# A hybrid attention and convolution layer: adaLN's first shift and scale by full precision products, later bias tables and convolution blocks, bias tiles read straight from the tables

## The chip, the cores and the metric

One core of a Trainium2 chip runs the kernel. The metric is the device time of one execution in microseconds; the kernel before took 2568.53 us, the median of three runs (2560.25 to 2570.44). All traces are of single executions on that core.

## What is computed

One layer of a diffusion backbone, in float32, for 2048 latent tokens of width 1024 and 256 context tokens. What matters here:

```python
mod_x = silu(c) @ w_ada + b_ada               # six rows of 1024: sh1, sc1, g1, sh2, sc2, g2
mod_c = silu(c_ctx) @ w_ada + b_ada
hx = rms_norm(x, norm1_g) * (1 + sc1) + sh1   # hc likewise from ctx, with mod_c
q, k, v, u = split(hx @ w_in)
attn = neighbourhood_attention(rope(q), q, rope(k), v, kc, vc, rpb)   # window + context keys, bias rpb
a, b = split(u); h = depthwise_conv31(a * sigmoid(b)) + dw_bias
conv = silu(layer_norm(h))
x = x + g1 * (concat(attn, conv) @ w_out)
x = x + g2 * (relu(modulate(rms_norm(x)) @ w1) ** 2 @ w2)
return rms_norm(x, final_g)
```

## The kernel before, in words

Every large product is made of three products of one pass (`mm3`, L89): each operand is split into a rounded part, made on ACT, and the rest, made by a subtraction on DVE or GpSimd (POOL in the profile); high times high, high times low and low times high are added in PSUM. PSUM is four tiles of 128 x 1024 (`psA`, L54), handed out in turn; a tile that is held longer is taken out of the turn.

**The head (L136 to L277).** The first two chunks of `w_ada`, shift and scale, come in four tiles of 2 MB each, in two loads each (`load_wada`); one row of `b_ada` each goes into `brow`. `silu(c)` and `silu(c_ctx)` are spread over 64 columns each, so one product with a 128 x 128 stationary matrix gives both rows on 64 partitions. First each bias row is multiplied with a row of ones at full precision (L193), then `ada_step` (L196) runs 8 times for the scale (`hf` 1) and 8 times for the shift: ACT casts 128 x 1024 of `w_ada`, DVE or POOL subtracts, and PE does six products of 512 columns. Between the shift's steps DVE builds `Ar` from the scale's PSUM and scales the first x tiles (L244, L251). After the last product the shift is copied out and added to the x tiles (L664 to L673), and PE transposes these (`trans`, L224, L227) for the projection.

**The projection (L559 to L881).** Two blocks of 1024 tokens; in each 10 groups of columns of `w_in` (4 `u`, 2 `q`, 2 `k`, 2 `v`), each in two halves of 512 tokens. So there are 40 steps: for the first block u is steps 0 to 7, q 8 to 11, k 12 to 15, v 16 to 19, for the second u 20 to 27, q 28 to 31, k 32 to 35, v 36 to 39. A step's products are 10.9 to 11.5 us of PE at the full clock. `half` (L710) emits a step: products, then what they need after: for u a sigmoid gate stored to `h_d`, for q and k the rotary work (`rope_store`: DVE, ACT, POOL, an `m1` buffer of two, stores), for v the split and stores (`v_tiles`). Beside this, the same function issues at fixed steps:

- the convolution by blocks of 98 tokens (`Conv`, L418), through a transform of length 128: `load` of 128 rows of `h_d` (`cw`), `split` (ACT, DVE), `fwd` (three products; `y` = PSUM times a table on DVE, into SBUF; `cyh` on ACT, `cyl` on DVE), one step later `inv` (six products, bias, statistics), two steps later `turn` (four transposes, activation, store). One PSUM tile is held for this. Block 0 enters at step 7 and one block at each further step to 16; blocks 10 to 20 enter at steps 27 to 37.
- the relative bias tables: `bias_start` and `bias_end` at step 6, one head in each of steps 8 to 15 (`bias_head`: two loads, a POOL add, four stores into `tf_d` and `ti_d`), and at steps 18, 20, 21 and 24 `bias_rows` (L302), which copies shifted pieces of both into `bias_d` in DRAM, 12 copies in all.
- the second x half of each block: loads, squares on ACT, scaling on DVE, shift on POOL (`norm_half`, L545), transposes (`trans_half`). For the second half of the second block the norm stands at step 20 and the transposes at step 22.
- three gate chunks of `w_ada` (`ada_chunk`, L484): 16 loads of 256 KB and 16 accumulations on DVE each, taken from a queue at a budget of 5.2 a step (0.6 each) in u steps, and `finish`, two steps after the last, which sums over partitions on PE, loads the bias row and adds it.

A planner orders the instructions of each engine by program order and a timeline of its own; where `in_order` is called, DVE, ACT and POOL keep the order written. All DMAs of these parts are issued on SP's queue.

**Attention (L898 to L1235).** 64 steps of 128 queries and two heads (4 pairs of heads, 8 groups of 4 rows, 2 halves of the columns). At each step `loads` issues k, q and v three or two steps ahead, and `load_b` (L998) one bias tile of 128 rows per head whenever the kind of group changes, 48 in all; eight of these at the start.

The output projection and the MLP follow; they are not touched.

## Time and profile before

| | us |
|---|---|
| median of three runs | 2568.53 |
| the profiled execution, its own time | 2570.69 |
| its span, first to last instruction | 2568.9 |
| PE busy in the span | 2430.5 |
| DVE, ACT, POOL busy | 1790.2, 1248.7, 1467.8 |

The span is divided as follows: head to about 52 us, projection to about 665, attention to about 940, then output projection and MLP. The profile gives busy times by engine; the granted clock of TensorE is 1.00 at 2.4 GHz and 0.50 at 1.2 GHz, and a stretch between these has had both. In the timeline a row in square brackets tells the idle time ahead and what ended it.

### The profile page before, as it was taken

To read this page: it belongs to the slowest core of one execution; us is meant where nothing else is said; L and a number is where in the kernel's file an instruction comes from. 1 tells how busy PE (TensorE), PEld (TensorE's weight loads), DVE (VectorE), ACT (ScalarE), POOL (GpSimd) and SP (SyncE) were. 2 spreads that over 40 slices of the span, in tenths; PEclk is the share of its full clock that TensorE was granted. 3 is DMA by queue.
4 is the path that set the end of the run, shared out by engine and by line. 5 is a ranking of instruction groups with operands and counts; after the bars stand their busy time and mean duration, and the time that the engine had idled before them with its cause. 6 is when DMAs were issued, how large, how long until landed. Compare 5 with 4: busy or idle time off the path is not lost.

```text
span 2568.9 us, 42313 instructions
## 1 busy us (share of the span) xinstructions
PE 2430.5 (95%) x15903; PEld 2216.9 (86%) x15903; DVE 1790.2 (70%) x2465; ACT 1248.7 (49%) x2162; POOL 1467.8 (57%) x1055
## 2 busy tenths in 40 slices
PE   7997989899889999988999999999999999999997
PEld 5985889689889999987998889999889998799996
DVE  6646743666689976468666697666786676876676
ACT  4334531443689963134444554444554445454442
POOL 3537422442578856457555676555675556755564
PEclk9998999999999999999999999999999999999999
DMA  8555764653899865665333443333343334433321
GB/s 299 158 168 163 223 216 130 196 154 110 227 253 262 241 182 174 195 231 165 99 99 107 129 139 111 101 105 99 121 148 101 99 99 126 137 107 100 105 92 57
DMA packets 293882, 387.26 MB, mean 151 GB/s; under 512 B 38021, under 2 KB 231228, under 8 KB 293644
## 3 DMA queue, kind: packets, MB, share of 16 engines
q1 hardware_dynamic: 293660, 384.54, 49.7%
q8 instruction: 125, 2.05, 0.3%
q14 instruction: 81, 0.66, 0.1%
q10 hardware_dynamic: 16, 0.00, 0.0%
HBM read 308.03 MB, written 86.76 MB: 154 GB/s over the span
## 4 chain that ended last, share of the span: by engine, by line
PE 62%; DVE 10%; DMA 9%; POOL 5%; issue 4%; SPq 2%; ACT 1%; DVEq 0%; POOLq 0%; ACTq 0%
PE pall L90 18%; PE pall L91 18%; PE pall L92 18%; PE pall L1105 2%; PE pall L1069 1%; PE pall L1030 1%; DVE s L1398 1%; DMA ar<-at_d 1%; DVE ac L1501 1%; DVE ac L1497 1%; PE pall L1107 1%; DVE w L1423 1%; PE pall L1032 1%; DMA cw<-h_d 1%; DMA xn_d<-xo 1%
## 5 line engine op out<-in xcount | busy, mean ns | idle before, releaser
L90 PE MATMUL pall<-w,hh 128*128 128x512 f32 x1024 | 406.0, 397 | 11.0 <-DVE ac L1497 7.2
L91 PE MATMUL pall<-w,hh 128*128 128x512 f32 x1024 | 403.0, 394 | 0.0
L92 PE MATMUL pall<-w,hl 128*128 128x512 f32 x1024 | 397.2, 392 | 0.6 <-DVE hl L1454 0.6
L1497 DVE TENSOR_TENSOR ac<-pall,ac 128x1024 f32<-128x1024 f32 x239 | 286.8, 1214 | 73.9 <-PE pall L92 73.2
L90 PEld LDWEIGHTS pall<-w,hh 128*128 128x128 f32 x1024 | 195.1, 190 | 51.6 <-issue 4.4
L92 PEld LDWEIGHTS pall<-w,hl 128*128 128x128 f32 x1024 | 193.3, 189 | 41.9 <-DVE hl L1454 2.2
L91 PEld LDWEIGHTS pall<-w,hh 128*128 128x128 f32 x1024 | 194.8, 190 | 36.4 <-issue 0.2
L1451 ACT ACTIVATE c<-c 128x512 f32<-128x512 f32 x128 | 80.9, 632 | 157.2 <-DVE c L1471 129.2
L86 POOL TENSOR_TENSOR w_0l<-w_0r,w_0h 128x1024 fp32r<-128x1024 f32 x20 | 50.7, 2537 | 172.7 <-ACT w_0h L85 152.5
L90 PE MATMUL pall<-xah,w 128*128 128x256 f32 x512 | 144.8, 284 | 4.7 <-ACT w L1392 4.7
L92 PE MATMUL pall<-xah,w 128*128 128x256 f32 x512 | 145.2, 284 | 0.0
L91 PE MATMUL pall<-xal,w 128*128 128x256 f32 x512 | 145.0, 283 | 0.0
L1454 DVE TENSOR_TENSOR hl<-c,hh 128x512 fp32r<-128x512 f32 x128 | 123.7, 967 | 15.3 <-ACT hh L1453 15.2
L1062 POOL TENSOR_SCALAR sb<-sb,ri 128x696 f32<-128x696 f32 (+1 forms) x128 | 105.6, 826 | 49.7 <-DVE ri L1057 40.7
L1044 DVE CUSTOM_DVE_ANT_0 sb<-pall,bias 128x696 f32<-128x696 f32 (+1 forms) x128 | 108.0, 845 | 6.5 <-PE pall L1032 5.9
L1052 ACT ACTIVATE sb<-sb,mn 128x696 f32<-128x696 f32 (+1 forms) x128 | 109.6, 857 | 0.6 <-DVE mn L1044 0.6
L90 PEld LDWEIGHTS pall<-xah,w 128*128 128x128 f32 x512 | 98.1, 192 | 7.5 <-ACT w L1392 4.9
L91 PEld LDWEIGHTS pall<-xal,w 128*128 128x128 f32 x512 | 98.6, 192 | 2.8
L92 PEld LDWEIGHTS pall<-xah,w 128*128 128x128 f32 x512 | 98.6, 192 | 2.1
L90 PE MATMUL pall<-xth,w 128*128 128x256 f32 x256 | 75.2, 294 | 19.1 <-DVE pu L1459 19.1
L1105 PE MATMUL pall<-pw,v 120*128 120x256 f32 (+1 forms) x480 | 90.8, 309 | 0.8 <-ACT ob L1112 0.8
L1081 DVE TENSOR_TENSOR pw<-pall,pw 120x512 fp32r<-120x512 f32 (+1 forms) x128 | 83.5, 653 | 5.1 <-ACT pw L1076 4.7
(853 smaller groups left out, 8797.0 us busy)
## 6 DMA issues: line engine op xcount, KB each, us to landing
v<-v_d SPq DMA_DIRECT2D x144, 120.0 KB
q<-q_d SPq DMA_DIRECT2D x64, 256.0 KB
wr<-in_w_ada SPq DMA_DIRECT2D x48, 256.0 KB
v_d<-vt SPq DMA_DIRECT2D x64, 160.0 KB
wa<-in_w_ada SPq DMA_DIRECT2D x8, 1024.0 KB
x<-in_x SPq DMA_DIRECT2D x16, 512.0 KB
kr<-k_d SPq DMA_DIRECT2D x32, 256.0 KB
at_d<-ao SPq DMA_DIRECT2D x32, 256.0 KB
```

Source lines behind the costliest of these rows:

```text
L86: (eng or GE).tensor_tensor(l, r, f(h), ALU.subtract)
L90: TE.matmul(outp, lh, rh, start=start, stop=False)
L91: TE.matmul(outp, lh, rl, start=False, stop=False)
L92: TE.matmul(outp, ll, rh, start=False, stop=stop)
L1044: VE.tensor_tensor_reduce(sb[:, c0:SE_], d["s"][:, 512 - SC0 + c0:768], bt[:, c0:SE_], -1.0, 3e38, ALU.add, ALU.min, mn)
L1052: SE.activation(pb[:, c0:SE_], pb[:, c0:SE_], AF.Exp, bias=d["mn"], scale=-1.0, accum_out=d["sm"])
L1062: GE.tensor_scalar(pb[:, c0:SE_], pb[:, c0:SE_], d["ri"], 1.0, ALU.mult, ALU.mult)
L1081: VE.tensor_tensor(pw[0:120, 0:nch, 1, :], d["tv"], f(pw)[0:120, 0:nch, 0, :], ALU.subtract)
L1105: TE.matmul(o, VT[(pr, *key)][0:n, hd, :], pw[0:n, ch, :, :], start=(ch == 0), stop=False)
L1451: SE.activation(c, c, AF.Relu)
L1454: VE.tensor_tensor(dl, cv, f(dh), ALU.subtract)
L1497: VE.tensor_tensor(ac, po_, ac, ALU.add)
```

## The change

It does six things. (1) The head's products take `silu(c)` and `w_ada` as they are, in float32 at full precision, two instructions for each of the 16 steps, with no casts and subtractions of `w_ada`; the bias rows are split instead, and added by products of one pass (`ada_bias`). (2) The convolution's blocks enter by a table of steps (`ENTER`): 0 to 7 at steps 12 to 19, 8 at 22, 9 at 24, 10 to 20 at 27 to 37 as before; u steps can run `inv` and `turn` too. (3) `y` lies in a PSUM tile of the common turn. (4) The bias tables start at step 17 (`G0 - 2` is group 8) and are made in steps 20 to 27; `bias_d` and its 12 copies are gone, and `load_b` reads a bias tile by four loads of 32 rows out of `tf_d` or `ti_d`. (5) A gate chunk's bias row is loaded with the last accumulation. (6) The last half's odd x tiles are shifted on DVE.

```diff
-    silh = pa.tile([P, KD, P], F32R, tag="cos", name="silh")
-    sill = pa.tile([P, KD, P], F32R, tag="sin", name="sill")
...
-    VE.tensor_copy(sv_[0], silb)
-    VE.tensor_tensor(sv_[1], silb, f(sv_[0]), ALU.subtract)
+    silr = pa.tile([P, KD, P], F32, tag="cos", name="silr")
+    VE.tensor_copy(silr.rearrange("p k (j n) -> p k j n", j=2), silb)
+    brh, brl = ([wtile(f"br{z}{hf}")[0:1] for hf in range(2)] for z in "hl")
+    onesr = wtile("onesr")[0:1, 0:P]
+    VE.tensor_copy(onesr, ones[0:1, :])
     for hf in (1, 0):
+        SE.copy(brh[hf], brow[hf])
+        VE.tensor_tensor(brl[hf], brow[hf], f(brh[hf]), ALU.subtract)
+
+    def ada_bias(hf):
         for n in range(2):
-            TE.matmul(pm[hf][:, n * 512:(n + 1) * 512], ones[0:1, :], brow[hf][:, n * 512:(n + 1) * 512],
-                      start=True, stop=False)
+            sl = slice(n * 512, (n + 1) * 512)
+            TE.matmul(pm[hf][:, sl], onesr, brh[hf][:, sl], start=True, stop=False)
+            TE.matmul(pm[hf][:, sl], onesr, brl[hf][:, sl], start=False, stop=False)
 
     def ada_step(hf, k):
         src = wts[hf, k // 4][:, k % 4, :]
-        wh, wl = wtile(f"wah{k}{hf}"), wtile(f"wal{k}{hf}")
-        SE.copy(wh, src)
-        (GE if k % 3 == 1 else VE).tensor_tensor(wl, src, f(wh), ALU.subtract)
         for n in range(2):
             sl = slice(n * 512, (n + 1) * 512)
-            o = pm[hf][:, sl]
-            TE.matmul(o, silh[:, k, :], wh[:, sl], start=False, stop=False)
-            TE.matmul(o, sill[:, k, :], wh[:, sl], start=False, stop=False)
-            TE.matmul(o, silh[:, k, :], wl[:, sl], start=False, stop=(k == KD - 1))
+            TE.matmul(pm[hf][:, sl], silr[:, k, :], src[:, sl], start=False, stop=(k == KD - 1))
...
-    def bias_rows(i):
-        for ty, t, o, n in ((0, tf_d, 7 - i, 320), (1, ti_d, 3 - i, 440), (2, tf_d, 3 - i, 320)):
-            SY.dma_start(bias_d[ty][:, i], t.rearrange("h f c n -> (h f) c n")[:, :, o * 40:o * 40 + n])
...
-            y = pa.tile([P, 2, 512], F32, tag="acc", bufs=2, name=f"cy{i}")
+            y = psA(f"cy{i}").rearrange("p (z n) -> p z n", z=2)
...
+    def conv_at(d):
+        i = ENTER.get(now[0] - d)
+        if i is not None:
             (Conv.inv, Conv.turn)[d - 1](cvs[i])
...
             if i == 2 * KD:
+                box["b"] = pa.tile([1, D], F32, tag="m1", bufs=2, name=f"br{ch}")
+                SY.dma_start(box["b"], a["b_ada"][:, ch * D:(ch + 1) * D])
                 pe_todo.append(finish)
...
-            shift(i)
+            shift(i, VE if b and hf and i % 2 else GE)
...
+    ENTER = {n: i for i, n in enumerate([*range(12, 20), 22, 24, *range(27, 38)])}
...
             for t in range(4):
+                if t % 2 == 0:
+                    conv_at(2 - t // 2)
...
-        if gi == 3 and hf == 0:
+        if gi == G0 - 2 and hf == 1:
             bias_start()
             bias_end()
-        if 4 <= gi < 8:
-            bias_head((gi - 4) * 2 + hf)
+        if G0 <= gi < G0 + 4:
+            bias_head((gi - G0) * 2 + hf)
...
-        SY.dma_start(bt[:, SC0 - nw:SC0], bias_d[ty][h * 2 + hf].rearrange("i c n -> (i c) n"))
+
+        t, o = ((tf_d, 7), (ti_d, 3), (tf_d, 3))[ty]
+        for i in range(4):
+            SY.dma_start(bt[i * 32:i * 32 + 32, SC0 - nw:SC0], t[h, hf][:, (o - i) * 40:(o - i) * 40 + nw])
```

## Rows read from the trace of the kernel before

**Rows 1.** The page, busy time of each engine: us, share of the span, instructions.

```profile
PE 2430.5 (95%) x15903; PEld 2216.9 (86%) x15903; DVE 1790.2 (70%) x2465; ACT 1248.7 (49%) x2162; POOL 1467.8 (57%) x1055
```

**Rows 2.** Stretches of 20 us: engine busy times, granted clock, DMA share, GB/s.

```profile
0.00:20.00 20.00, 14.07 (x24) 7.35 (x25) 6.99 (x8) 7.70 (x9) 5.51 (x8) 1.00 0.90 344
...
200.00:220.00 20.00, 15.96 (x64) 12.61 (x65) 13.31 (x19) 13.30 (x27) 14.15 (x12) 0.91 0.68 187
220.00:240.00 20.00, 15.16 (x68) 11.88 (x66) 11.33 (x15) 8.04 (x17) 13.83 (x5) 0.93 0.39 99
240.00:260.00 20.00, 10.94 (x30) 8.00 (x31) 15.21 (x9) 7.72 (x13) 18.39 (x12) 0.56 0.57 169
260.00:280.00 20.00, 20.00 (x92) 16.33 (x91) 18.82 (x20) 9.15 (x14) 10.41 (x6) 1.00 0.70 185
...
300.00:320.00 20.00, 18.18 (x145) 17.50 (x144) 8.61 (x17) 11.34 (x20) 2.04 (x1) 1.00 0.96 319
...
360.00:380.00 20.00, 15.02 (x116) 14.20 (x115) 10.83 (x8) 9.34 (x14) 8.60 (x3) 0.93 0.37 106
380.00:400.00 20.00, 18.68 (x136) 18.66 (x135) 5.18 (x5) 5.63 (x6) 6.43 (x4) 0.82 0.05 14
...
420.00:440.00 20.00, 20.00 (x169) 20.00 (x168) 10.54 (x11) 3.19 (x4) 5.22 (x2) 1.00 0.48 133
...
480.00:500.00 20.00, 11.83 (x47) 7.24 (x46) 15.74 (x24) 10.92 (x22) 17.71 (x10) 0.92 0.64 193
```

**Rows 3.** Timeline of PE in the head: start, duration, operation, count, idle time ahead.

```profile
6.18 3.75 PE L193 MATMUL pall<-brow,ones 1*128 1x512 f32 x4 [3.42 <-DMA brow<-in_b_ada]
...
42.55 1.17 PE L206 MATMUL pall<-wal,silh 128*128 128x512 f32 x2 [2.69 <-DVE wal L200]
...
46.50 0.39 PE L204 MATMUL pall<-wah,silh 128*128 128x512 f32 x1
...
47.66 0.39 PE L206 MATMUL pall<-wal,silh 128*128 128x512 f32 x1
51.83 0.66 PE L227 MATMUL pall<-ident,x 128*128 128x128 f32 x4 [3.78 <-DVE x L666]
```

**Rows 4.** The tile `wa`, operations on it: ns least, median, most; first and last start.

```profile
L199 ACT CAST wah<-wa x16: 1032/1044/1055, 6.4 to 36.9; 128x1024 fp32r<-128x1024 f32 x16
L200 DVE TENSOR_TENSOR wal<-wa,wah x10: 1209/1612/3389, 7.5 to 43.8; 128x1024 fp32r<-128x1024 f32 x10
...
L200 POOL TENSOR_TENSOR wal<-wa,wah x6: 2358/2428/3403, 8.5 to 38.0; 128x1024 fp32r<-128x1024 f32 x6
```

**Rows 5.** Timeline of PE in the MLP: the gate's two products at full precision.

```profile
1401.23 1.88 PE L1370 MATMUL pall<-fg,ones 128*128 128x512 f32 x4
```

**Rows 6.** Timeline of DVE in the head: two scalings of x tiles.

```profile
46.12 4.21 DVE L251 SCALAR_TENSOR_TENSOR x<-x,ss,Ar 128x1024 f32<-128x1024 f32 x2
```

**Rows 7.** Timelines of PE, DVE and POOL about the longest wait in the q steps.

```profile
251.94 0.74 PE L91 MATMUL pall<-cyl,chl 128*98 128x512 f32 x1 [6.50 <-DVE cyl L439]
...
242.54 9.34 DVE L439 TENSOR_TENSOR cyl<-cy,cyh 128x1024 fp32r<-128x1024 f32 x1 [5.82 <-ACT cyh L438]
...
240.18 9.27 POOL L221 TENSOR_TENSOR x<-x,Br 128x1024 f32<-128x1024 f32 x4
```

**Rows 8.** Timelines of DVE and POOL: norm of the last x half.

```profile
370.04 9.04 DVE L218 SCALAR_TENSOR_TENSOR x<-x,n11ss,Ar 128x1024 f32<-128x1024 f32 x4
...
371.40 12.20 POOL L221 TENSOR_TENSOR x<-x,Br 128x1024 f32<-128x1024 f32 x4 [18.04 <-DVE x L218]
```

**Rows 9.** Stretches of 20 us, as rows 2, at attention's first change of heads.

```profile
720.00:740.00 20.00, 15.66 (x123) 15.18 (x122) 15.46 (x42) 14.54 (x33) 13.95 (x23) 0.97 1.04 247
```

**Rows 10.** Waits from 455 to 505 us: who for whom, us, times, longest.

```profile
PE pall L90 <- DVE br L518: 5.3, 1, 5.3
```

**Rows 11.** The tile `bias`: its loads in attention, ns least, median, most.

```profile
L1008 SPq DMA_DIRECT2D bias<-bias_d x48: 326/353/1444, 651.9 to 879.2; - x48
```

**Rows 12.** Waits from 640 to 690 us.

```profile
DVE kt L842 <- DMA kr<-k_d: 4.2, 1, 4.2
```

More of the change, by code (lines that the diff above doesn't have):

```diff
@@ L111, in hybrid_layer @@
     ti_d = dr.tile([8, 2, 32, 14 * 40], F32, name="ti_d")
-    bias_d = [dr.tile([16, 4, 32, n], F32, name=f"bias_d{i}") for i, n in enumerate((320, 440, 320))]
     ident = const.tile([P, P], F32, name="ident")
@@ L251, in scale0 @@
         VE.scalar_tensor_tensor(x0[i], x0[i], ss0[:, i:i + 1], Ar, ALU.mult, ALU.mult)
+    ada_bias(1)
     for k in range(KD):
         ada_step(1, k)
+    ada_bias(0)
     TE.transpose(pk[:, 144:152], vrow, ident[:8, :8])
@@ L464, in hybrid_layer, with conv_end @@
     cvs = [Conv(i) for i in range(NCB)]
-    cv_pos = [0]
-    def conv_at(d, last):
-        i = cv_pos[0] - d
-        if 0 <= i < last and not hasattr(cvs[i], f"did{d}"):
-            setattr(cvs[i], f"did{d}", True)
+    now = [0]
+    def conv_at(d):
+        i = ENTER.get(now[0] - d)
+        if i is not None:
             (Conv.inv, Conv.turn)[d - 1](cvs[i])
-    def conv_end(last):
-        i = cv_pos[0]
-        if i < last:
+    def conv_end():
+        i = ENTER.get(now[0])
+        if i is not None:
             cvs[i].split()
             cvs[i].fwd()
-            if i + 1 < last:
-                cvs[i + 1].load()
-        cv_pos[0] += 1
+        i = ENTER.get(now[0] + 1)
+        if i is not None:
+            cvs[i].load()
     def ada_chunk(ch):
@@ L515, in finish @@
                           start=True, stop=True)
-            br = pa.tile([1, D], F32, tag="m1", bufs=2, name=f"br{ch}")
-            SY.dma_start(br, a["b_ada"][:, ch * D:(ch + 1) * D])
+            br = box["b"]
             VE.tensor_tensor(br, pg[0:1, :], br, ALU.add)
@@ L679, in hybrid_layer @@
     NG = len(groups)
-    CB0 = (BLK - P + PAD) // CL + 1
-    CBS = (CB0, NCB)
-    BR0 = 9
+    G0 = NG // NB
+    ENTER = {n: i for i, n in enumerate([*range(12, 20), 22, 24, *range(27, 38)])}
+    assert len(ENTER) == NCB
     adas = {ch: ada_chunk(ch) for ch in (2, 3, 4)}
-    G0 = NG // NB
     ADA = {G0 - 1: 2, G0: 3, G0 + 2: 4}
@@ L727, in half @@
             SY.dma_start(h_d[t0:t0 + 512, ct * P:(ct + 1) * P].rearrange("(t p) c -> p t c", p=P), sg)
-            if ct == 3 and hf == 1:
-                cv_pos[0] = (0, CB0)[b]
-                cvs[cv_pos[0]].load()
-                conv_end(CBS[b])
+            conv_end()
         elif kind in "qk":
@@ L734, in half @@
             for j in range(2):
-                conv_at(2 - j, CBS[b])
+                conv_at(2 - j)
                 for k in range(KD):
@@ L739, in half @@
             rope_store(b, kind, idx, hf, pt)
-            conv_end(CBS[b])
+            conv_end()
         else:
@@ L746, in half @@
                 row = (b * BLK + hf * 512 + t2 * 256) // W
-                conv_at(2 - t2, CBS[b])
+                conv_at(2 - t2)
                 if idx == 1 and hf == 1 and b + 1 < NB:
@@ L750, in half @@
                 v_tiles([getter(2 * t2), getter(2 * t2 + 1)], row, wget, idx, f"{b}{idx}{hf}{t2}")
-            conv_end(CBS[b])
+            conv_end()
         if gi == 1 and hf == 0:
@@ L784, in half @@
             conv_tables()
-        if hf == 0 and BR0 <= gi < BR0 + 4:
-            bias_rows(gi - BR0)
         todo, pe_todo[:] = list(pe_later), list(pe_todo)
@@ L858, in hybrid_layer @@
     for i, (gi, hf) in enumerate(steps):
+        now[0] = i
         for nxt, nh in steps[i + 1:i + 3]:
```

1 line of the change is left out of this document (removed).

## The prediction

> **What bounds the kernel now.** I read the page's busy shares first: TensorE is busy for 95% of the span [rows 1], so elsewhere only what makes PE wait, or runs it at the lower clock, can be won. Next comes the table by stretches of 20 us, to find where PE is not busy. In the projection it shows three dips: 200 to 260 us, 380 to 400 us and 480 to 500 us [rows 2]. In 200 to 260 PE is busy 15.96 + 15.16 + 10.94 = 42.1 of 60 us, and the granted clock is 0.91, 0.93 and 0.56. Full is 2.4 GHz and the lower level 1.2 GHz, so 0.56 means the lower level for 88% of that stretch. A busy microsecond at the lower level does half a microsecond of work: 0.88 x 10.94 / 2 = 4.8 us there, and some 3 us in the two stretches before. With 17.9 us of idle time that stage loses about 26 us. At 380 to 400 it is 1.3 us idle and about 3.4 us of clock, with 5 us more idle and 1 us of clock just ahead; at 480 to 500 it is 8.2 us idle. Third, the timeline of the head: PE runs the first modulation products until 48.0 us and transposes the first x tile at 51.83 [rows 3]. From there PE is nearly full, so what the head saves or costs reaches the end. Last, attention: where the head pair changes, PE is busy for 15.66 of 20 us with the DMA engines at 1.04 [rows 9].
>
> **The head.** Removed are 16 ACT casts, 10 DVE and 6 POOL subtractions [rows 4] and 96 products of one pass; added are 32 products at full precision. PE's waits for subtractions (2.69 us before 42.55, the longest [rows 3]) go with them. Such a product shows as two records: four records, two products of 128x128 by 128x512, took 1.88 us at the full clock [rows 5], so with the pipeline's tail taken off about 0.44 us a record, 28 us for 64. At the lower clock the bias products show 3.75 us for four [rows 3], about 0.9 us a record. When does it start? The bias row has landed at 6.18; a cast of 1.04 and a subtraction of 1.2 (lengths as for w_ada's [rows 4], the free size being the same) give 8.4, four short bias products 10.1. The clock is low then; after the idle time before 42.55 it took until 46.50 for records of one pass to come down to 0.39 us [rows 3], 4 us. I allow 4.5 us, five records, then 59 x 0.44 = 26, then 1 us for the other bias: the end is at about 41.5 instead of 48.0. DVE's two scalings, which ran to 50.33 [rows 6], come earlier because DVE is free; what stood behind them until 51.83 (copy, add) is 1.5 us. So the first transpose comes at about 43.4: **-8 us**. Next in line would be w_ada's transfer: at 344 GB/s [rows 2] 6.9 MB are in at 20 us, and the 9.5 MB up to its last part (8 of w_ada, 1 of x, 0.5 of the norm's gain) by about 28, when the second half's products begin. Bounds: -10 if the clock rises at once, +19 if it never does (10.1 + 64 x 0.9 + 2, then 1.5: 71 against 51.8).
>
> **Convolution and biases in the first block of 1024 tokens.** Blocks 0 to 9 of the convolution move from steps 7 to 16 to steps 12 to 19, 22 and 24; inverse and transpose follow one and two steps later as before. The 8 bias heads (two loads and four stores on SP and one POOL add each) move from steps 8 to 15 to 20 to 27, the start of the biases from 6 to 17. PE's idle time in 200 to 260 stands before convolution products, in five places; the longest waits 6.50 us for `cyl`, which took DVE 9.34 us while POOL added a shift for 9.27 us [rows 7]. With `y` in PSUM that subtraction has one operand left in SBUF, and with the blocks gone the q steps have DVE for the rotary work alone. Where do the blocks go? The k steps already hold convolution at 260 to 280 without idle time, the v steps at 300 to 320 with 1.8 us, the copies of the bias rows beside them (DMA 0.96) [rows 2]. The u steps at 420 to 440 have half of DVE and three quarters of POOL free [rows 2]. So of 26 us I take **-20**, with -10 and -26 as ends, and for the new crowding in v and u steps **+4**, from 0 to +12 (a wait like the old ones, 17.9 / 5 = 3.6 us, for three blocks). `y` also takes one of three free PSUM tiles: the next step's `y` waits for the evacuation of the projection before it, on DVE and ACT, whose queues hold that evacuation ahead of `y`; a step of about 11 us covers it, so nothing; uncovered it is the same crowding.
>
> **The second x half.** Its four shifts on POOL end at 383.6, after DVE's scalings, and PE's transposes wait [rows 8]. Twelve copies of 640 and 880 KB go from SP and from the DMA engines just ahead of those x loads, and two of the four shifts go to DVE. About 10 us are lost at 360 to 400 (idle 6.3, clock 4) [rows 2]; I take **-7**, ends -2 and -10. The four scalings beside POOL's adds took 9.04 us, 2.26 each, where DVE's subtractions of that size take from 1.2: the two engines hinder each other [rows 4, 7, 8]. The Trainium skill (SBUF — State Buffer, Who interferes with whom) says that a VectorE instruction with two SBUF inputs and a GpSimd one that reads SBUF exclude each other for a whole instruction; the two shifts moved to DVE are of that kind, so by it they would save about 3 us of the chain, not 6, and the term would be -4.
>
> **The gate's bias row.** PE waits 5.3 us behind the third chunk's add, which waits for a load asked for only then [rows 10]; now it is asked for two steps earlier: **-5**, ends -2 and -8. It holds one of two `m1` buffers meanwhile, so a q step's rotary multiply on DVE could wait for the store, and the projection two steps on for its PSUM; at most the 5.3 us come back.
>
> **Bias tiles in attention.** 48 loads become 192 of a quarter of the size, the same bytes and rows. An issue takes SP 0.353 us [rows 11]: 144 more are 51 us, hidden where SP has time. At the entry eight tiles are 24 more issues, 8.5 us; the next head's k load is queued behind four of them, and DVE already waits 4.2 us for it [rows 12]. At each of three changes of head pair twelve tiles, 36 more issues, 12.7 us, fall in about 25 us of steps. What is late then is q and v, and PE. I take +4 for the entry and +2 for each change, **+10**; ends 0 (all hidden) and +20 (the entry's 8.5 and 4 a change). The Trainium skill (DMA: Bandwidth & Descriptors, Measured (HBM→SBUF)) says that transfers under 64 KB are dominated by descriptors; the loads go from 160 and 220 KB to 40 and 55 KB. No run here shows it for these loads, whose row count stays; by it the upper end, +20, would hold, 2555.
>
> **The sum.** -8 - 20 + 4 - 7 - 5 + 10 = -26 us. The profiled run took 2570.69, its span 2568.9, and the median of the runs shown is 2568.53, 2 us less; from the profiled run I come to **2545**. All lower ends together give 2517, all upper ends 2579, and 2608 with the head at the lower clock throughout.
>
> **Rivals.**
> *The products stay at the lower clock.* Against it: PE got back to the full clock after 4 us of dense work [rows 3]. For it: it was at the lower level through the bias products, the only full precision work in the head. Price: +19 for -8, so 2572.
> *The stalls travel with the convolution (slower).* Place: DVE's queue in steps 16 to 25, where a u step adds some 9 accumulations (5.2 of budget at 0.6 each) of the gate chunk and step 20 four scalings and two shifts ahead of `cw`, `cy`, `cyl`. If all ten blocks then wait 3.6 us as five did (36, and 8 for the clock), 44 stand for 26: +18 in place of -16, and the x half gains nothing. With the head's -8, the row's -5 and attention's +10 that is +15, 2586. It decides from some 6 stalled blocks. Against it: DVE at 420 to 440 is busy 10.5 of 20 [rows 2].
> *SP is the bound of attention.* If nothing of 51 us of issue is hidden at entry and changes of head: 8.5 + 3 x 7 = 30 instead of 10, so 2565. For it: PE dips to 15.66 of 20 at the first change already [rows 9].
> *The head gives nothing*, w_ada landing as late as it is used now: 2553; inside the forecast's range.
>
> **How the numbers follow.** Forecast 0.68, own range 2526 to 2558; lower clock 0.10; travelling stalls 0.10; SP 0.12. About 0.5%, 13 us, is what a measurement of this kernel can tell from no change: faster is below 2555.7, slower above 2581.4. Faster: nearly all of the forecast, 0.66; same: the lower clock, SP, the forecast's edge, 0.24; slower: the travelling stalls, 0.10. 2522 to 2572 holds the forecast, SP and half of the lower clock, 0.8.
>
> **What would show it.** Right: L227's first transpose near 43 us; the 64 product records in some 30 us; no PE wait on `cyl` or `cyh` in the q steps; granted clock near 1.0 in 200 to 260; no wait on `br`; the entry into attention some 4 us longer. Wrong: product records in over 50 us; waits on `cw`, `cy` in v and u steps; PE waiting on q or kr for over 5 us at a change of head pair.

## The result, and the profile after

The change makes the kernel slower: 2594.12 us (median of 4 runs, 2588.33 to 2597.45) against 2569.49 us for the kernel before on the same chip, ratio 1.01, 95% interval 1.0069 to 1.0131. The prediction was 2545, faster, with 2522 to 2572 as its range. The profiled run after took 2593.83 us, its span is 2592.0. The page's busy times, as in [rows 1]:

```profile
PE 2441.9 (94%) x15871; PEld 2218.9 (86%) x15871; DVE 1762.0 (68%) x2459; ACT 1250.6 (48%) x2158; POOL 1441.6 (56%) x1047
```

PE's busy time grew by 11 us and the span by 23. Two marks on PE's timeline divide the span: the first score product (it opens attention) and the last product with the context's v (it closes it). First the kernel before, then after:

```profile
665.95 0.53 PE L1030 MATMUL pall<-kt,q 128*128 128x320 f32 x2 [0.67 <-DMA q<-q_d]
...
940.10 0.63 PE L1107 MATMUL pall<-pc,vc 128*128 128x256 f32 x2
```

```profile
652.04 0.53 PE L1027 MATMUL pall<-kt,q 128*128 128x320 f32 x2 [2.54 <-DMA q<-q_d]
...
962.89 0.63 PE L1104 MATMUL pall<-pc,vc 128*128 128x256 f32 x2
```

Up to the first mark the kernel won 13.9 us; attention went from 274.8 to 311.5 us, +36.7; what follows is the same within half a microsecond. -13.9 + 36.7 = +23.

**The head** came as predicted. PE's timeline after, which answers to [rows 3]:

```profile
9.57 9.85 PE L204 MATMUL pall<-wa,silr 128*128 128x512 f32 x16
...
20.54 20.87 PE L204 MATMUL pall<-wa,silr 128*128 128x512 f32 x48
42.66 0.66 PE L225 MATMUL pall<-ident,x 128*128 128x128 f32 x4 [1.26 <-DVE x L662]
```

The 64 records (two for each product) took 30.7 us, the first 16 of them 9.85 us and the last 48 0.435 us each, and ended at 41.41; the first transpose stands at 42.66 instead of 51.83.

**The projection** won next to nothing behind that (the new head alone brings the first mark to 652.0 too, see before_head): its waits changed hands. After, DVE, POOL and PE near 200 us (three timelines):

```profile
200.35 11.77 DVE L216 SCALAR_TENSOR_TENSOR x<-x,n10ss,Ar 128x1024 f32<-128x1024 f32 x4
212.05 0.74 DVE L603 TENSOR_TENSOR ql0q<-pall,qh0q 128x256 fp32r<-128x256 f32 x2
...
204.44 9.91 POOL L219 TENSOR_TENSOR x<-x,Br 128x1024 f32<-128x1024 f32 x3
...
212.51 0.79 PE L90 MATMUL pall<-t01h,w_0h 128*128 128x512 f32 x1 [8.91 <-DVE ql0q L603]
```

Before, it was `cyl` of the convolution that ran beside POOL's adds and made PE wait 6.50 us [rows 7]. Now the convolution is gone from these steps, and the four scalings of the same norm run beside the adds; the last read of a projection's PSUM (`ql0q`) stands behind them on DVE, and PE waits 8.91 us for it.

**Attention** lost time where bias tiles are loaded: at the entry and at each change of head pair. First all of attention, between the two marks (columns as in [rows 2]), before and after:

```profile
665.95:940.73 274.78, 256.63 (x1985) 250.07 (x1986) 248.19 (x633) 236.73 (x513) 209.77 (x311) 0.98 0.91 237
```

```profile
652.04:963.52 311.48, 269.42 (x1985) 260.80 (x1986) 248.27 (x632) 236.11 (x512) 208.69 (x309) 0.92 0.80 210
```

PE's idle time goes from 18.1 to 42.1 us. The other 13 us stand in longer products: the same 1985 records take 269.4 us instead of 256.6, at a granted clock of 0.92 instead of 0.98. Stretches of 20 us after:

```profile
660.00:680.00 20.00, 13.58 (x94) 12.90 (x92) 10.54 (x28) 9.34 (x21) 7.20 (x12) 0.83 0.76 212
...
720.00:740.00 20.00, 13.67 (x95) 12.80 (x93) 11.85 (x35) 12.63 (x31) 11.33 (x20) 0.91 0.64 167
740.00:760.00 20.00, 12.71 (x85) 12.11 (x85) 10.31 (x26) 8.81 (x20) 6.67 (x10) 0.83 0.91 227
...
820.00:840.00 20.00, 17.17 (x103) 16.54 (x104) 14.20 (x36) 11.26 (x24) 11.55 (x17) 0.74 1.04 248
...
880.00:900.00 20.00, 13.04 (x85) 12.15 (x85) 9.11 (x25) 10.24 (x24) 6.67 (x12) 0.89 0.78 219
```

PE is idle for 29.8 of these 100 us. The DMA engines' share is 0.64 to 0.91 but for one stretch, and over all of attention it fell from 0.91 to 0.80: nothing in these rows shows the DMA engines short of time. The tile `bias`, its loads after (in place of [rows 11]), and then SP's timeline at a change with the PE row that it delays:

```profile
L1005 SPq DMA_DIRECT2D bias<-tf_d x128: 302/419/1745, 636.1 to 928.2; - x128
...
L1005 SPq DMA_DIRECT2D bias<-ti_d x64: 302/419/1662, 655.6 to 891.8; - x64
```

```profile
726.49 3.62 SPq L1005 DMA_DIRECT2D bias<-tf_d  x8
...
733.01 3.90 SPq L1005 DMA_DIRECT2D bias<-ti_d  x8
737.01 0.38 SPq L960 DMA_DIRECT2D q<-q_d  x1
737.44 1.41 SPq L984 DMA_DIRECT2D v<-v_d  x3
738.95 0.38 SPq L1120 DMA_DIRECT2D at_d<-ao  x1
739.42 4.90 SPq L1005 DMA_DIRECT2D bias<-ti_d  x8
744.42 0.38 SPq L960 DMA_DIRECT2D q<-q_d  x1
...
747.58 0.68 PE L1027 MATMUL pall<-kt,q 128*128 128x440 f32 x2 [3.70 <-DMA q<-q_d]
```

A step of attention (64 of them in 274.8 us before) lasts 4.3 us. Eight bias loads take SP 3.6 to 4.9 us; q, v and the store of the output come on top. From 733.01 to 744.80 no gap between SP's rows is longer than 0.1 us (before, between 725 and 735 us, there are gaps of 0.3 to 1.0 us): here SP is the engine that sets the step. The waits of attention show it at PE and behind PE; before and after:

```profile
POOL sb L1062 <- DVE ri L1057: 40.7, 62, 6.2
ACT pw L1076 <- PE pall L1069: 19.0, 48, 1.9
```

```profile
POOL sb L1059 <- DVE ri L1054: 82.2, 67, 12.0
ACT pw L1073 <- PE pall L1066: 52.1, 51, 8.4
PE pall L1027 <- DMA q<-q_d: 22.4, 11, 3.7
```

### The profile page after: what moved, and what is told of

Read it like the earlier page. It is cut to its first block, busy times and chain, and to the rows that moved or that the text cites. A ratio compares the mean times of both kernels' runs of the same rounds, so it can differ in the third digit from the quotient of the medians.

```text
span 2592.0 us, 42352 instructions
## 1 busy us (share of the span) xinstructions
PE 2441.9 (94%) x15871; PEld 2218.9 (86%) x15871; DVE 1762.0 (68%) x2459; ACT 1250.6 (48%) x2158; POOL 1441.6 (56%) x1047
## 4 chain that ended last, share of the span: by engine, by line
PE 66%; DVE 9%; DMA 7%; issue 4%; POOL 3%; SPq 2%; ACT 1%; DVEq 0%; ACTq 0%; POOLq 0%
PE pall L90 20%; PE pall L92 19%; PE pall L91 19%; PE pall L1102 2%; PE pall L1066 1%; DMA q<-q_d 1%; PE pall L1027 1%; DVE s L1395 1%; DVE ac L1498 1%; DVE ac L1494 1%; DMA wr<-in_w_ada 1%; PE pall L1104 1%; DMA cw<-h_d 1%; PE pall L1029 1%; DVE w L1420 1%
## 5 line engine op out<-in xcount | busy, mean ns | idle before, releaser
L1073 ACT CAST pw<-pall 120x512 fp32r<-120x512 f32 (+1 forms) x128 | 72.6, 568 | 64.2 <-PE pall L1066 52.1
L1066 PE MATMUL pall<-ident,sb 128*120 128x128 f32 x480 | 78.5, 286 | 18.4 <-DVE pc L1094 8.3
L1027 PE MATMUL pall<-kt,q 128*128 128x440 f32 (+1 forms) x256 | 73.1, 368 | 22.7 <-DMA q<-q_d 22.4
```

What stands on the lines that cost most here:

```text
L1027: TE.matmul(s[:, 512 - nw:512], q[:, hd, 1, :], win, start=(z == 0), stop=(z == 1))
L1066: TE.transpose(t[0:120, ch * P:(ch + 1) * P], pb[:, c0 + 120 * ch:c0 + 120 * ch + 120], ident)
L1073: SE.copy(d["pw"][0:120, 0:nch, 0, :], d["tv"])
```

## The experiments

One table for all; the ratio is to the kernel before on the same chip. "First" is the start of the first score product, "attention" the time from there to the last product with the context's v. Each mark is read from one profile, and a profiled run lies up to 8 us from its kernel's median (oldbias_noshift: 2572.55 against 2580.85), so a few us between two marks show nothing by themselves.

| kernel | us | ratio (95%) | first | attention |
|---|---|---|---|---|
| before | 2569.49 | 1 | 665.9 | 274.8 |
| after | 2594.12 | 1.0100 (1.0069 to 1.0131) | 652.0 | 311.5 |
| before_four | 2603.28 | 1.0135 (1.0118 to 1.0152) | 662.2 | 310.4 |
| before_split4 | 2601.67 | 1.0135 (1.0106 to 1.0163) | 665.0 | 310.5 |
| one_load | 2623.55 | 1.0214 (1.0193 to 1.0235) | 666.7 | 327.2 |
| act_issue | 2602.49 | 1.0126 (1.0109 to 1.0143) | 657.2 | 318.7 |
| after_qfirst | 2589.12 | 1.0078 (1.0057 to 1.0099) | 650.6 | 305.0 |
| after_copies | 2582.32 | 1.0050 (1.0035 to 1.0065) | 675.6 | 278.3 |
| before_head | 2557.65 | 0.9955 (0.9940 to 0.9971) | 652.0 | 276.1 |
| after_oldbias | 2577.67 | 1.0026 (1.0008 to 1.0044) | 670.6 | 279.1 |
| h_ypsum | 2560.48 | 0.9967 (0.9953 to 0.9980) | 656.1 | 278.0 |
| h_shift | 2560.08 | 0.9967 (0.9951 to 0.9983) | 655.8 | 276.3 |
| h_row | 2557.44 | 0.9951 (0.9932 to 0.9970) | 649.3 | 278.9 |
| h_move | 2556.11 | 0.9951 (0.9934 to 0.9969) | 651.8 | 276.6 |
| oldbias_ysbuf | 2551.50 | 0.9919 (0.9904 to 0.9934) | 647.6 | 277.4 |
| oldbias_noshift | 2580.85 | 1.0038 (1.0025 to 1.0050) | 671.6 | 276.9 |
| after_ysbuf | 2584.43 | 1.0061 (1.0039 to 1.0083) | 640.9 | 306.8 |
| h_norm | 2552.27 | 0.9926 (0.9911 to 0.9941) | 645.0 | 276.5 |
| h_norm_move | 2555.70 | 0.9936 (0.9922 to 0.9951) | 650.3 | 276.3 |
| best | 2545.99 | 0.9916 (0.9893 to 0.9940) | 645.1 | 274.9 |

### What attention pays for

**before_four.** The kernel before, whose `load_b` is that of after; the twelve copies go.

```diff
-        SY.dma_start(bt[:, SC0 - nw:SC0], bias_d[ty][h * 2 + hf].rearrange("i c n -> (i c) n"))
+        t, o = ((tf_d, 7), (ti_d, 3), (tf_d, 3))[ty]
+        for i in range(4):
+            SY.dma_start(bt[i * 32:i * 32 + 32, SC0 - nw:SC0], t[h, hf][:, (o - i) * 40:(o - i) * 40 + nw])
```

> The kernel before with nothing but the bias loads of after: the twelve copies dropped, four loads of 32 rows for a tile. Theory: attention 275 + 37 = 305 to 315 us, the dropped copies give the projection 0 to 5 us, the time 2569.5 + 37 - 2 = 2604 (2598 to 2610). Rival, attention suffers from what the projection leaves behind: the projection is that of before, so attention stays at 275 to 285 and the time within 2560 to 2578.

The time and both marks came as the theory had them: attention +35.6 us, and in this profile the first mark is 3.7 us earlier, put down to the dropped copies. So the loads alone cost attention its time.

**before_split4.** The contiguous tables of before, but four loads for a tile.

```diff
-        SY.dma_start(bt[:, SC0 - nw:SC0], bias_d[ty][h * 2 + hf].rearrange("i c n -> (i c) n"))
+        src = bias_d[ty][h * 2 + hf].rearrange("i c n -> (i c) n")
+        for i in range(4):
+            SY.dma_start(bt[i * 32:i * 32 + 32, SC0 - nw:SC0], src[i * 32:i * 32 + 32])
```

> The kernel before, whose bias tiles are still read from their own contiguous tables, but in four loads of 32 rows. Theory (the number of issues is the price): attention 305 to 315 us as with the four loads from the raw tables, the time 2606 (2598 to 2612). Rival, the price lies in reading rows that are not contiguous: attention 275 to 282 us, the time 2566 to 2577.

The same +35.7 us, so rows with a stride are not the price. The issue has the same length, and PE the same wait (tile `bias`, and waits in attention):

```profile
L1010 SPq DMA_DIRECT2D bias<-bias_d x192: 302/419/1930, 649.1 to 941.5; - x192
```

```profile
PE pall L1032 <- DMA q<-q_d: 20.0, 10, 3.9
```

**act_issue.** The kernel after; ScalarE issues the bias loads.

```diff
-            SY.dma_start(bt[i * 32:i * 32 + 32, SC0 - nw:SC0], t[h, hf][:, (o - i) * 40:(o - i) * 40 + nw])
+            SE.dma_start(bt[i * 32:i * 32 + 32, SC0 - nw:SC0], t[h, hf][:, (o - i) * 40:(o - i) * 40 + nw])
```

> The kernel after with its 192 bias loads issued by ScalarE instead of SP: the same transfers, the same rows, another queue. Theory (SP's issue): SP is as free as before; attention 275 to 290 us, the upper part if ScalarE's own issue delays exponentials and copies; the time 2558 to 2572. Rival, 192 small transfers as such cost the DMA engines' time: attention 300 or more, the time 2585 or more.

The theory missed: attention is 7 us longer than after, and the rival's numbers came (300 or more, 2585 or more). But the rows give another reason for them. An issue takes ScalarE 0.31 to 0.34 us, and 192 of them stand in the queue that holds the exponentials, for which DVE's reciprocal now waits (after: 8.5 us):

```profile
L1005 ACTq DMA_DIRECT2D bias<-tf_d x128: 308/340/1822, 640.2 to 914.0; - x128
...
L1005 ACTq DMA_DIRECT2D bias<-ti_d x64: 308/309/523, 652.1 to 901.1; - x64
```

```profile
DVE ri L1054 <- ACT sb L1049: 45.7, 21, 10.3
```

PE's wait for q fell from 22.4 to 3.6 us, as it must if SP was free. I had taken an issue as nearly free on ScalarE; here the engine that issued paid. By itself the run does not decide between the theory and the rival, and no run here makes 192 small loads without their issues standing on an engine that attention needs.

**one_load.** The raw tables are stored four times over (`i` of 4), so that a row stride lets one load read a whole tile.

```diff
-            src = tb[hf * 32:hf * 32 + 32, :, :].rearrange("p r c -> p (r c)")
-            SY.dma_start(tf_d[q, hf], src)
...
+            src = tb[hf * 32:hf * 32 + 32, :, :].rearrange("p r c -> p (r c)").unsqueeze(1).broadcast_to([32, 4, 600])
+            SY.dma_start(tf_d[q, hf].rearrange("i c n -> c i n"), src)
...
-        for i in range(4):
-            SY.dma_start(bt[i * 32:i * 32 + 32, SC0 - nw:SC0], t[h, hf][:, (o - i) * 40:(o - i) * 40 + nw])
+        src = t[h, hf, 0][:, o * 40:o * 40 + nw]
+        src = bass.AP(src.tensor, src.offset, [[32 * t.shape[-1] - 40, 4], *[list(s) for s in src.ap]])
+        SY.dma_start(bt[:, SC0 - nw:SC0], src)
```

> The kernel after, but the raw bias tables are stored four times over, so that one load with a row stride reads a whole bias tile: 48 loads instead of 192, the same 128 rows of the same length in each tile, no copies. Theory, SP's issue is what attention pays for: from the first score product to the end of attention 271 to 279 us instead of 311 (before 275), the time 2594 - 37 = 2557 (2552 to 2562). Rival, the small rows themselves or the DMA engines: rows and bytes are those of after, so attention stays at 305 or more and the time at 2588 or more. Rival, attention suffers from what the projection leaves behind: also 2585 or more.

The theory missed: 48 loads, and attention at 327 us is the longest of all. The rivals' numbers came (305 or more, 2588 or more), but for neither rival's reason: the transfers themselves are no longer those of after. The tile `bias`, and the longest wait of attention (before: 9.6 us for the same pair):

```profile
L1006 SPq DMA_DIRECT2D bias<-tf_d x32: 508/556/2223, 650.0 to 929.5; - x32
L1006 SPq DMA_DIRECT2D bias<-ti_d x16: 522/558/2172, 668.4 to 916.5; - x16
```

```profile
POOL ao L1119 <- DMA at_d<-ao: 52.0, 11, 7.1
```

SP has time again, but the transfers are late: from the end of the issue to the last packet a tile of 1280-byte rows takes 6.8 us (median, from the packet records) and one of 1760-byte rows 8.4, where each of the four loads of after takes 1.4 and the contiguous load of before 3.7 (3.3 and 4.6 by row length). The stores of the output behind them on the queue land late as well, and POOL waits for them. The Trainium skill (DMA: Bandwidth & Descriptors, Rules for kernel authors) says that a transfer runs on no more DMA engines than its slowest dimension has elements. Here that dimension is 4, so each engine would get 32 rows; a row took 70 and 87 ns (mean), which gives 2.2 and 2.8 us, an estimate, against 2.6 and 3.6 us from a tile's first packet to its last. That agrees in size; which engines ran no trace of this case shows. But it is the smaller part: the first packet of a tile came 3.9 and 4.7 us after the end of its issue (before: 1.5 and 2.2), and what held it is open. So this run says nothing for or against SP's issue as the price.

**after_qfirst.** Only SP's order within a step of attention.

```diff
-            for hd in range(2):
-                load_b(*groups_[p + 3], hd)
-        if 0 < p < NP - 3:
-            load_q(*groups_[p + 3])
+            if p > 0:
+                load_q(*groups_[p + 3])
         if 0 < p < NP - 2:
             load_v(*groups_[p + 2])
+        if p + 3 < NP:
+            for hd in range(2):
+                load_b(*groups_[p + 3], hd)
```

> The kernel after with SP's order within a step changed: the q and v loads are asked for ahead of the bias loads instead of behind them. If the price is only that q stands behind the bias loads: PE's 22 us of waits on q go, attention 280 to 295 us, the time 2562 to 2578. If SP's total time at the changes of head pair is the price, the wait only changes its place, to the bias tiles: attention 303 or more, the time 2585 or more.

Attention gets 6.5 of its 36.7 us back, and time and attention lie where the second reading had them. PE's wait for q falls from 22.4 to 12.5 us, and DVE's for the next head's k, asked for last, grows from 7.1 to 20.0. The wait changed its place, as it does if SP's total at these steps is the price and not the place of one load.

**after_copies** and **after_oldbias.** The kernel after with the bias tiles of before; first with the heads at the steps of after and the copies two steps behind them, then with both at the steps of before. Shown is part of after_oldbias's edit:

```diff
+    bias_d = [dr.tile([16, 4, 32, n], F32, name=f"bias_d{i}") for i, n in enumerate((320, 440, 320))]
+    def bias_rows(i):
...
-        if G0 <= gi < G0 + 4:
-            bias_head((gi - G0) * 2 + hf)
+        if 4 <= gi < 8:
+            bias_head((gi - 4) * 2 + hf)
+        if hf == 0 and 9 <= gi < 13:
+            bias_rows(gi - 9)
```

> The kernel after with the bias tiles of the kernel before: twelve copies build the tiles' own tables, two steps after the last bias head, and one contiguous load fills a tile. Theory (SP's issue): attention back to 272 to 280 us, the copies cost the v and u steps 0 to 8 us, the time 2557 to 2566. Rival, rows and transfers: the same. Rival, attention suffers from what the projection leaves behind: attention 300 or more, the time 2585 or more.

> The kernel after with everything about the bias tiles as before: heads at the steps of before, the twelve copies at the steps of before, one contiguous load for a tile. The head, the moved convolution, y in PSUM, the two shifts and the early bias row stay. Theory (the 192 loads cost attention 36 us, the rest of the change gains): first score product at 652 (648 to 657) us, attention 274 to 280 us, the time 2594 - 37 = 2557 (2550 to 2564). Rival, the bias work of the first block collides there with the convolution that was moved beside it: first score product at 662 or later, the time 2567 or more.

Attention is back at 278 and 279 us in both, as the theory had it. But the times missed it, by 16 and 14 us: both projections are some 20 us longer than that of after. For after_copies the theory had allowed 0 to 8; for after_oldbias the rival had named it (662 or later, 2567 or more). In after_copies the copies meet the loads of the second block: from 480 to 500 us PE is busy for 5.11 of 20 us with the DMA engines at 1.01, and PE's longest wait of the projection, 18.1 us, is for the convolution's `cw`. In after_oldbias the copies stand where they stood before; whether the cause is the bias work, as the rival said, or another part of the change, the next runs look for.

### What the projection pays for

**before_head.** The kernel before with the two hunks of the head alone, from `silr` to `ada_step`, and the calls:

```diff
+    ada_bias(1)
     for k in range(KD):
         ada_step(1, k)
+    ada_bias(0)
```

> The kernel before with nothing but the new head. Theory: the first transpose of x at 42 to 43.5 us instead of 51.8, and all of it reaches the end: 2570 - 9 = 2561 (2556 to 2565). Rival, a later wait of the projection takes it back: first transpose as said, but the first score product within 4 us of 666 and the time 2566 to 2573.

The head's gain reaches the end: -11.5 us. It is more than the 9.2 us of the first transpose; behind it PE idles 13.1 us between 200 and 260 us instead of 17.9. And the first score product stands at 652.0 us, where it stands in the kernel after too: all the rest of the change together gave the projection nothing.

**h_ypsum, h_shift, h_row, h_move.** before_head and one more part of the change each; of h_move only the table `ENTER` and what reads it.

```diff
-            y = pa.tile([P, 2, 512], F32, tag="acc", bufs=2, name=f"cy{i}")
+            y = psA(f"cy{i}").rearrange("p (z n) -> p z n", z=2)
```

```diff
-            shift(i)
+            shift(i, VE if b and hf and i % 2 else GE)
```

```diff
+                box["b"] = pa.tile([1, D], F32, tag="m1", bufs=2, name=f"br{ch}")
+                SY.dma_start(box["b"], a["b_ada"][:, ch * D:(ch + 1) * D])
                 pe_todo.append(finish)
```

```diff
+    ENTER = {n: i for i, n in enumerate([*range(12, 20), 22, 24, *range(27, 38)])}
```

> The kernel before with the new head (2557.7, first score product at 652.0 us) and y of the convolution in PSUM, nothing else. If the old stalls in the q steps came from DVE's operands in SBUF beside POOL's adds: about half of the 18 us of idle time and of the clock's loss in 200 to 260 goes, first score product at 640 to 646, the time 2546 to 2552. Rival, the stall goes on to the next link of the chain (the cast, the scalings, the shifts): first score product at 649 to 655, the time 2554 to 2561.

> The kernel before with the new head and, of the rest, nothing but two of the four shifts of the last x half on DVE. The prediction's term would give -7, the time 2551; by two engines that hinder each other -4, 2554; rival, DVE is itself the late one there: the idle time changes its place, 2556 to 2562.

> The kernel before with the new head and, of the rest, nothing but the early load of the gate's bias row. The prediction's term would give -5, the time 2553, and no wait on br; rival, another wait of the same stretch ends last, 2556 to 2560.

> The kernel before with the new head and, of the rest, nothing but the convolution's blocks at the steps of after; y in SBUF, the bias work, the shifts and the row as before. Theory (the stalls travel with the blocks and meet the twelve copies in the same steps): first score product at 664 to 676 us, the time 2570 to 2583. Rival, the prediction's term: first score product at 636 to 645, the time 2541 to 2550.

Each is within 3 us of before_head's 2557.65: in the first three the rival's time came true, and h_move fell between its two cases. PE's waits in the projection show how each stall was handed on: before_head, h_ypsum, h_shift, and h_move with one row of DVE's timeline.

```profile
PE pall L90 <- ACT cyh L440: 8.8, 2, 5.2
PE pall L91 <- DVE cyl L441: 7.7, 2, 6.5
PE pall L227 <- POOL x L221: 6.1, 3, 2.6
PE pall L90 <- DVE br L520: 5.2, 1, 5.2
```

```profile
PE pall L460 <- DVE pall L437: 11.5, 2, 9.8
PE pall L813 <- DVE ql1q L609: 7.7, 1, 7.7
```

```profile
PE pall L227 <- DVE x L221: 4.2, 1, 4.2
...
PE pall L227 <- POOL x L221: 2.0, 1, 2.0
```

```profile
PE pall L90 <- ACT cyh L442: 10.2, 2, 9.9
...
205.12 13.82 DVE L219 SCALAR_TENSOR_TENSOR x<-x,n10ss,Ar 128x1024 f32<-128x1024 f32 x4
```

With y in PSUM the waits on `cyh` and `cyl` fall to 3.1 and 3.3 us, and two new ones of 9.8 and 7.7 us come. With two shifts on DVE PE waits 4.2 + 2.0 = 6.2 us instead of 6.1. The early row takes 3.3 us off its wait (1.9 us are left), about what the first mark won, and nothing of it is seen in the time. In h_move the blocks are gone from the q steps, but the norm is not: its four scalings take 13.82 us beside POOL's adds, `cy` and `cyh` stand behind them, and PE idles 15.2 us between 200 and 260 us, against 13.1 in before_head.

**oldbias_ysbuf, oldbias_noshift.** after_oldbias with one part undone each.

```diff
-            y = psA(f"cy{i}").rearrange("p (z n) -> p z n", z=2)
+            y = pa.tile([P, 2, 512], F32, tag="acc", bufs=2, name=f"cy{i}")
```

```diff
-            shift(i, VE if b and hf and i % 2 else GE)
+            shift(i)
```

> after_oldbias (2577.7) with y of the convolution back in SBUF: head, moved blocks, two shifts, early row. If y's PSUM tile is what makes the parts together 20 us worse than each alone: first score product at 648 to 656, the time 2552 to 2561. If it is the shifts on DVE or the early row: first score product at 664 or later, the time 2570 to 2580.

> after_oldbias (2577.7) with all four shifts of the last x half on POOL again; y stays in PSUM. If y's PSUM tile is the cause: unchanged, 2572 to 2582. If the shifts on DVE are: 2552 to 2563.

y's PSUM tile is the cause: without it 2551.5, 26 us less; without the shifts nothing changes. In after_oldbias the scalings on DVE, and PE's longest wait:

```profile
207.35 13.64 DVE L219 SCALAR_TENSOR_TENSOR x<-x,n10ss,Ar 128x1024 f32<-128x1024 f32 x4
```

```profile
PE pall L90 <- DVE ql0q L611: 17.8, 1, 17.8
```

Three PSUM tiles go round. A projection step takes one, and with y each step that starts a block takes two; so the second k step takes the tile of the step only two before it. That tile's last reader, `ql0q`, stands on DVE behind the four scalings. In oldbias_ysbuf PE has no wait on `ql0q`, and its longest is 10.2 us, on `cyh`.

**after_ysbuf.** The same edit on the kernel after.

> The kernel after with y of the convolution back in SBUF, the 192 loads kept. If y's PSUM tile ate the projection's gain here too (PE waits 8.9 us for an evacuation behind the norm's scalings): first score product at 636 to 645 us instead of 652, attention still 305 to 315, the time 2582 (2576 to 2588). Rival, without the copies nothing is to be had: the stall passes to the convolution's splits, first score product at 649 to 656, the time 2589 to 2598.

As expected: the first mark goes from 652.0 to 640.9, the time falls by 10 us (the intervals of the two ratios just overlap), and attention stays at 306.8.

**h_norm, h_norm_move.** The norm of the second block's first x half from the third q step (step 10) to the first v step (step 16); on before_head and on h_move.

```diff
-        if b + 1 < NB and kind == "q" and idx == 1 and hf == 0:
+        if b + 1 < NB and kind == "v" and idx == 0 and hf == 0:
             norm_half(pend["x"], b + 1, 0)
```

> The kernel before with the new head, and the norm of the second block's first x half two steps pairs later: in the first v step instead of the second q step. Theory (one stall, of DVE's instructions with two operands in SBUF against POOL's four adds of this norm, whoever stands there): PE's idle time in 200 to 260 us falls from 13.1 to under 5 us and the clock there stays near 1, first score product at 638 to 646, the time 2544 to 2552. Rival, the adds hinder DVE as much in the v steps: first score product at 649 to 656, the time 2554 to 2561.

> The kernel with the new head, the convolution's blocks at the steps of after, and the norm in the first v step. If the prediction's gain from moving the blocks was there but eaten by the norm's stall: below h_norm, 2540 to 2547. If the blocks' place is worth nothing of itself: 2546 to 2560, no better than h_norm, since the v steps now hold blocks, norm and copies.

Stretches of before_head, then of h_norm:

```profile
200.00:220.00 20.00, 18.86 (x86) 15.11 (x85) 11.44 (x17) 13.71 (x27) 15.23 (x9) 1.00 0.60 167
220.00:240.00 20.00, 8.02 (x29) 5.34 (x28) 14.16 (x10) 6.28 (x13) 20.00 (x11) 0.74 0.52 149
240.00:260.00 20.00, 20.00 (x85) 16.08 (x84) 15.42 (x20) 9.61 (x13) 15.02 (x8) 0.92 0.67 183
```

```profile
200.00:220.00 20.00, 16.68 (x75) 12.86 (x75) 14.45 (x20) 11.11 (x21) 16.37 (x10) 1.00 0.83 218
220.00:240.00 20.00, 17.38 (x79) 13.90 (x78) 13.52 (x17) 11.84 (x21) 11.48 (x9) 1.00 0.66 191
240.00:260.00 20.00, 19.39 (x88) 15.55 (x87) 12.63 (x19) 9.06 (x13) 7.47 (x4) 1.00 0.54 140
```

The blocks of the convolution are where they were, and yet PE's idle time falls from 13.1 to 6.6 us (under 5 was expected) and the granted clock stays at its upper level: the larger part of the stall belonged to the norm. `cyl` still took 7.00 us at 260, beside other instructions of POOL. The time, 2552.3, sits at the edge of the theory's numbers, because the v steps lose most of it again: h_norm is 10.6 us ahead of before_head at the first product of the v steps (263.8 against 274.4) and 2.4 us at the first product of the second block (332.1 against 334.5), and over 200 to 320 us PE's idle time is 14.8 against 15.2. The other 4 to 5 us that it has at the first score product are won later, and no run separates what won them. h_norm_move is no better than h_norm; the blocks' place shows no gain of its own.

**best.** h_norm with the two shifts and the early row (the diffs above).

> The kernel before with the new head, the norm in the first v step, two of the four shifts on DVE and the early row of the gate; convolution, y and bias tiles as before. If these add up now that the large stall is smaller: the row 3 to 5 us and the shifts 0 to 3 us below h_norm (2552.3), 2545 to 2550. Rival, other waits of the same stretches end last: 2550 to 2556.

2545.99 us, a ratio of 0.9916 (0.9893 to 0.9940): 21 us less than the kernel before on the same chip, and 48 less than the kernel after by the medians. It keeps before's blocks, bias tiles and y in SBUF. That it beats h_norm is not shown: 6 us by the medians, which are from two chips, but 0.001 by the ratios, whose intervals overlap, and the first mark is the same (645.1 and 645.0). So the shifts and the row are not shown to be worth anything here either.

## Why the prediction was wrong, point by point

**The head: right.** -8 was forecast for the first transpose, it is -9.2; 0.44 us a record, it is 0.435; end of the products at 41.5, it is 41.41. That the end fits to 0.1 us is luck: the products began at 9.57 and not at 10.1, and their first 16 records took 9.85 us where five at 0.9 and eleven at 0.44 make 9.3. (The terms as written, 10.1 + 4.5 + 26 + 1, and 1.5 for copy and add, come to 43.1 and not 43.4.) By itself the head gives -11.5 us. The rival of the lower clock did not come: 0.435 us is the length at the upper level. (The clock of [rows 2] says 1.00 for 0 to 20 us of the kernel before, although records of one pass are 0.63 us long there and 0.39 later; the prediction went by the lengths.)

**Bias tiles in attention: the mechanism right, the size wrong.** This is the step that turned the sign: "+4 for the entry and +2 for each change, +10; ends 0 and +20" measured +36.7, and +35.6 as the only edit. Of the 49 us between 2545 and 2594 some 27 lie here; some 22 lie ahead of the first mark, where -36 was forecast and -13.9 measured. An issue took 0.419 us and not 0.353, and the 192 took 80 us by that median. The larger error was in "hidden where SP has time": I set 36 more issues against 25 us of steps, and did not add what SP already does in these steps, nor that q stands behind eight bias loads in each of them. With 3.6 to 4.9 us for eight loads in a step of 4.3 us, SP had no time left there to hide them in. The rival that SP is the bound, at 30 us and a chance of 0.12, is the case that the rows show, and even its price was low: it took 7 us a change, though by its own count a change has 12.7 us of issues, and 8.5 + 38 would be 47. That the number of loads is the price is shown by before_split4, where nothing else changed; that it is paid in SP's issue is read from SP's timeline and from where the waits went, and no run shows it alone. The rule that the prediction cited for small transfers gave the upper end, +20; its table was measured on loads issued from GpSimd. It is not what these runs show: each small load landed 1.4 us after its issue, and the share of the DMA engines fell. Nearer is another rule of the Trainium skill (DMA: Bandwidth & Descriptors, Rules for kernel authors), that two transfers to disjoint halves of the partitions are not worth making and one transfer over 128 partitions is to be used. The runs agree, with 36 us for four parts; the reason that the page gives, the shared DMA engines, no run here tests.

**Convolution and y: wrong, in two steps.** "With the blocks gone the q steps have DVE for the rotary work alone" failed: the norm of the next x half stayed there, and its scalings took 11.77 us beside POOL's adds. In before_head the adds come after them: there they took 4.87 us, and it was POOL that waited, with one add of a bias head at 6.52 us beside them and 1.46 us for the next. The stall is not a block's, it is that of whatever DVE instruction has two operands in SBUF while POOL adds; h_norm shows it by moving the norm and not the blocks, and h_move by moving the blocks and not the norm. The rule of the Trainium skill that the prediction used for the shifts alone (SBUF — State Buffer, Who interferes with whom) covers it, and the trace agrees: `cyl` with y in SBUF took 9.34 us beside POOL's adds, and 1.21 us with y in PSUM beside a subtraction on POOL (after, 219.1 us). Second, "y also takes one of three free PSUM tiles ... so nothing" failed: the evacuation does not stand ahead of y but behind the scalings. That tile costs 10 us in the kernel after and 26 with the old bias tiles. Instead of -16 the moved blocks gave -1.5 us by themselves, which is not clear of noise.

**The second x half and the gate's row: wrong.** -7 and -5 were forecast, each alone gave nothing clear of noise. Of the two values for the shifts, 6 us of the chain by the row and 3 by the rule of exclusion, none was seen; PE's waits there sum to 6.1 us before and 6.2 after, since the shifts that DVE takes over come after the scalings it has to do first. Most of the row's wait did go, as forecast (5.2 to 1.9 us), but the time did not follow; where it was lost no run shows.

**The sum.** Against the kernel before at the first mark: the head -13.9, the dropped copies -3.7, y's tile +11.1, and -7.4 for the rest together (moved blocks and bias heads, shifts, row: what is left from 665.9 to after_ysbuf's 640.9 behind the first two) make -13.9. The last is only a remainder: it takes the effects as adding up, and some of the head's -13.9 comes from the shorter stall behind it. Forecast for the same were -8 and -28. With the bias tiles of before and y in SBUF the change gives 2551.5. That this is near 2545 bears nothing out: without the +10 for bias tiles the other terms forecast 2535. (All upper ends, with the head at -8, come to 2581 and not 2579.)

**The rival of the travelling stalls** gave 2586 and the sign that came, but by luck: the time was lost in attention.

## What to carry to other kernels

Before one transfer is made into several, add up what the issuing queue already does in the steps where they fall: an issue took its engine 0.31 to 0.56 us here (medians of the bias loads), on SP and on ScalarE, and what is asked for behind it comes that much later. Before a stall is credited to the instruction that PE waits for, look at what ran beside it; if it is long because another engine holds it up, moving it hands the stall to the next one. A PSUM tile taken from a set that goes round can bring a wait for an evacuation a step closer, as `ql0q` did here.

## What was not expected of the hardware

One load with a slowest dimension of 4 was in 6.8 to 8.4 us after its issue (medians by row length), and 3.7 us after it when the same 128 rows were one contiguous block; it made attention longer (327 us) than four loads of 32 rows did (311). An issue took ScalarE 0.31 to 0.34 us, hardly less than SP (0.35 to 0.42 us for the bias loads of before and after). Four scalings of 128x1024 on DVE took from 4.87 to 13.82 us, by which POOL instructions ran beside them.
